# Storing the gates' running sums in DRAM by head instead of by chunk

## The chip, the cores and the metric

The kernel runs on one core of one Trainium2 chip. The metric is the device time of one execution in microseconds (us), the median of several runs. The profile quoted is of one further execution.

## What is computed

One step of a hybrid decoder layer for a prompt of 1024 tokens and eight sample tokens, with a model width of 1024 and 8 heads of 128. After a normalisation and modulation, one input projection feeds two branches: A, a gated short convolution, and B, a gated delta rule (conv on q, k and v, a decay per head and token, the delta rule, a gated norm). Both are projected, merged by gates, and go through one output projection. What the change touches is the decay in branch B, from the reference, cut:

```python
g = -exp(a_log) * softplus(alpha_raw + dt_bias)          # log decay, per token and head
...
gc = jnp.cumsum(g, axis=-1)                              # running sum within a chunk
causal = idx[:, None] >= idx[None, :]
decay = jnp.exp(jnp.where(causal, gc[..., :, None] - gc[..., None, :], -jnp.inf))
kb = k * beta[..., None]
a_mat = jnp.where(strict, einsum(kb, k) * decay, 0.0) + eye
sol = triangular_solve(a_mat, [v * beta, kb * exp(gc)])
attn_qk = einsum(q, k) * decay
q_dec = q * exp(gc)
# scan over the chunks: v_new = u - w S;  o = q_dec S + attn_qk v_new;  S = S exp(gc_last) + k_dec^T v_new
```

So each head needs its running sums twice: as a difference of every pair of tokens of a chunk (decay), and as a factor on q.

## The kernel before

The prompt is worked in 8 chunks (NC) of 128 tokens (C), for 8 heads (NH). Products with large weights run on TensorE (PE) as three products of split operands (xh, xl for the input, whi, wlo for the weights). The program has these stages: the start (norm, modulation); a long list of jobs, each one column block of 128 of the input projection, three groups of 344 columns accumulated in PSUM tiles pm_t; the products of branch A and of B's output; the output projection and the tail.

Branch B runs beside the list of jobs. Its work is written as generators ("strands"), one or more for each head, that are advanced in the gaps between the matmuls of the jobs (slot()). Which strand goes next, and so the order of instructions on each engine, is set while the program is built: the class Sched keeps an estimated clock for each engine, Paced charges each instruction an estimated cost to it, and a strand's next step is issued when its estimated time has come. For a DMA, Sched.dma charges a fixed time and one by bytes, whatever the shape of the transfer. On the chip each engine then works through its instructions in that order; an engine that waits for one instruction issues none behind it. All loads and stores but a few are issued on SP's queue (SY).

The running sums are made once, in ba_gen: a matmul with a triangle gives gc as 128 tokens x (8 chunks x 8 heads); a transpose on PE and a copy give gcr as 64 rows of 128 tokens; a DMA stores gcr to gsc, a DRAM scratch of 64 rows of 512 bytes (line 270). Two places read it for each head h through gc_rows(h), which makes 8 rows out of it and broadcasts them to all 128 partitions, 512 KB in SBUF:

- decay_gen (line 851) loads the tile DA; ACT adds the negative sum of the partition's own token to each of the 8 chunks (ACTIVATE DA<-DA,ngc, 8 for each head), DVE masks into DB and DA, ACT takes exponentials.
- delta_gen (line 982) loads the tile gcB; qd_gen takes its exponential on ACT and multiplies q by it on DVE.

delta_gen holds the rest of a head: the products of k and q; the inversion, whose blocks go through DRAM (sA, At, sT and back into Ts) with a long run of small DVE operations on Ts and Ttmp between; small products that finish the inverse (pa_t tiles with DB, Ts, T11); then the scan over the 8 chunks, in which PE, a DVE operation that writes X, PE again, an ACT copy that writes vn, and PE with vn follow each other. The PSUM tiles of branch B are pa_t, and the names in the profile are those of the tiles.

sample_gen, for the eight sample tokens, has a broadcast of the same size: it stores rT to rsc and reads it back to all partitions as rB, from one run of 4 KB in DRAM.

Of the kernel before, what the change touches and what calls it, by code (L numbers as in the profile page):

```python
# [8 lines left out]
F32 = mybir.dt.float32  # L9
# [7 lines left out]
P = 128  # L17
# [5 lines left out]
NH = 8  # L23
C = 128
NC = S // C
# [133 lines left out]
def hybrid_step(  # L159
# [9 lines left out]
    V, A, PE, GP, SY = (Paced(e, n, sched) for e, n in (  # L169
        (nc.vector, "V"), (nc.scalar, "A"), (nc.tensor, "PE"), (nc.gpsimd, "GP"), (nc.sync, "SY")))  # L170
# [9 lines left out]
    def ps_aux():  # L180
        return psum["pa"].tile([P, 512], F32, tag="pa", name="pa_t")

    def tt(out, a, b, op):
        V.tensor_tensor(out=out, in0=a, in1=b, op=op)

    def ts(out, a, s1, s2=None, op0=ALU.mult, op1=None):
        if s2 is None:
            V.tensor_scalar(out=out, in0=a, scalar1=s1, scalar2=None, op0=op0)
        else:
            V.tensor_scalar(out=out, in0=a, scalar1=s1, scalar2=s2, op0=op0, op1=op1)  # L190

    def stt(out, a, s, b, op0, op1):
        V.scalar_tensor_tensor(out=out, in0=a, scalar=s, in1=b, op0=op0, op1=op1)
# [6 lines left out]
    def act(out, in_, func, **kw):  # L200
        A.activation(out=out, in_=in_, func=func, **kw)
# [57 lines left out]
    gc = cpool.tile([P, NC, NH], F32, name="gc")  # L259
# [10 lines left out]
    gsc = dram.tile([NC * NH, C], F32, name="gsc")  # L270
# [11 lines left out]
    def transpose(out, in_):  # L282
        n = in_.shape[0]
        PE.transpose(out, in_, ident[:n, :n])
# [449 lines left out]
    def ba_gen():  # L734
        ap_ = bp
        ban = ap_.tile([P, 9, 16], F32, name="ban")
        GP.memset(ban, 0.0)
        pt = ps_aux()
        for i in range(9):
            n = P if i < 8 else NB  # L740
            transpose(pt[:n, 48 * i:48 * i + 48], ba[:, i * P:i * P + n])
        for n, i0, i1 in ((P, 0, 8), (NB, 8, 9)):
            pv = pt[:n, 48 * i0:48 * i1].rearrange("p (i n) -> p i n", n=48)
            V.tensor_copy(out=ban[:n, i0:i1, :], in_=pv[:, :, 0:16])
            tt(ban[:n, i0:i1, :], ban[:n, i0:i1, :], pv[:, :, 32:48], ALU.add)
        T4.give(ba_)
        al = ap_.tile([P, NH], F32, name="al")
        db = ap_.tile([P, NH], F32, name="db")
        SY.dma_start(out=al, in_=a_log.to_broadcast([P, NH]))
        SY.dma_start(out=db, in_=dt_bias.to_broadcast([P, NH]))  # L750
        act(beta, ban[:, :, 0:NH], AF.Sigmoid)
        yield
        xg = ap_.tile([P, 9, NH], F32, name="xg")
        u = ap_.tile([P, 9, NH], F32, name="u")
        sq = ap_.tile([P, 9, NH], F32, name="sq")
        pl = ap_.tile([P, 9, NH], F32, name="pl")
        tt(xg, ban[:, :, NH:16], db.unsqueeze(1).to_broadcast([P, 9, NH]), ALU.add)
        act(al, al, AF.Exp)
        stt(u, xg, -1.0, xg, ALU.mult, ALU.max)
        act(u, u, AF.Exp, scale=-1.0)  # L760
        ts(sq, u, 2.0, op0=ALU.add)
        V.reciprocal(out=sq, in_=sq)
        tt(u, u, sq, ALU.mult)
        tt(sq, u, u, ALU.mult)
        ts(pl, sq, 1.0 / 19)
        for n in (17, 15, 13, 11, 9, 7, 5, 3):
            stt(pl, pl, 1.0 / n, sq, ALU.add, ALU.mult)
        stt(pl, pl, 1.0, u, ALU.add, ALU.mult)
        ts(xg, xg, 0.0, op0=ALU.max)
        stt(xg, pl, 2.0, xg, ALU.mult, ALU.add)  # L770
        stt(xg, xg, -1.0, al.unsqueeze(1).to_broadcast([P, 9, NH]), ALU.mult, ALU.mult)
        yield

        pt = ps_aux()
        gv = xg[:, 0:8, :].rearrange("p c h -> p (c h)")
        PE.matmul(pt[:, 0:64], lhsT=triu, rhs=gv, start=True, stop=True)
        PE.matmul(pt[:, 64:128], lhsT=ones, rhs=gv, start=True, stop=True)
        gcf = gc.rearrange("p c h -> p (c h)")
        V.tensor_copy(out=gcf, in_=pt[:, 0:64])
        neg["gc"] = ngc = ap_.tile([P, NC, NH], F32, name="ngc")  # L780
        ts(ngc.rearrange("p c h -> p (c h)"), gcf, -1.0)
        tt(ekd.rearrange("p c h -> p (c h)"), pt[:, 64:128], gcf, ALU.subtract)
        act(egl.rearrange("p c h -> p (c h)"), pt[:, 64:128], AF.Exp)
        act(ekd, ekd, AF.Exp)
        act(egc, gc, AF.Exp)
        yield
        pt = ps_aux()
        transpose(pt[:64, 0:C], gcf)
        gcr = ap_.tile([64, C], F32, name="gcr")
        V.tensor_copy(out=gcr, in_=pt[:64, 0:C])  # L790
        SY.dma_start(out=gsc, in_=gcr)
        act(u[:NB, 0, :], xg[:NB, 8, :], AF.Exp)
        SY.dma_start(out=smp[0], in_=u[:NB, 0, :])
        SY.dma_start(out=smp[1], in_=beta[:NB, 8, :])
        SY.dma_start(out=gbs.rearrange("p a b h -> p (a b h)"),
                     in_=smp.rearrange("a b h -> (a b h)").unsqueeze(0).to_broadcast([P, 2 * NB * NH]))
        flags["ba"] = True
# [43 lines left out]

        jobs.append((w_in, c0, P, x_src, None, evac, after))

    gc_rows = lambda h: gsc.rearrange("(c h) i -> h c i", h=NH)[h].unsqueeze(0).to_broadcast([P, NC, C])
    waiting = set()

    def decay_gen(h, st):
# [968 lines left out]
    for g0, gn in GROUPS:  # L1816
# [5 lines left out]
        A.copy(out=ba[:, g0:g0 + gn], in_=ps[:48, :gn])  # L1822
    T4.give(wb_)
    start(ba_gen())
    run(jobs, 1, isp)
    products()
# [30 lines left out]
    for j in range(9):  # L1857
        i, n, xr, mh, ml, held = pre.pop(j)
# [33 lines left out]
        for half in range(2):  # L1892
            hs = slice(half * 512, (half + 1) * 512)
            stt(yt[:n, hs], yt[:n, hs], r, xr[:n, hs], ALU.mult, ALU.add)
            out = y_prompt[0, i * P:(i + 1) * P, hs] if i < 8 else y_sample[:, 0, hs]
# [38 lines left out]
```

## Time and profile before

| | |
|---|---|
| median of 3 runs | 1454.48 us (1453.16 to 1454.57) |
| the profiled execution | 1455.76 us; span from first to last instruction 1454.1 us |
| PE busy in the span | 1401.6 us, 96% |
| DVE, ACT, POOL busy | 994.0 us (68%), 673.0 us (46%), 38.2 us (3%) |
| mean granted clock of PE | 0.979 |
| DMA packets | 200271, of which 175774 under 2 KB; 165.99 MB |
| loads of DA and gcB from gsc | 8 and 8, 512 KB each |
| where they are issued | DA from 91.0 to 656.1 us, gcB from 126.3 to 689.4 us |

PE's busy time is that of pipelined matmuls and hides short waits. A wait that the profile lists is idle time of an engine, put down to what ended last before the instruction that follows. In rows of the profile every instruction has line 126, the helper that issues them, so tiles tell them apart. SPq is SP's instruction stream, which issues DMAs; a row of it is the issue, not the transfer.

### The profile page before, as it was taken

What the parts mean: (1) busy time and instruction counts of PE and PEld (TensorE: products, weight loads), DVE (VectorE), ACT (ScalarE), POOL (GpSimd) and SP (SyncE); (2) the same over time, 40 slices, a digit from 0 to 9 for tenths busy, and PEclk for the clock granted to TensorE, in tenths of its full rate; (3) what the DMA queues carried; (4) which work ended last, traced back from release to release, by engine and by line L of the source; (5) the groups of instructions that cost most, each with busy time, mean ns of one, the idle gap of its engine ahead of it and who ended that gap; (6) DMA issues with size and microseconds to landing.
All of it is one profiled execution on the core that took longest, in us unless ns stands there. A gap on an engine that the chain in (4) does not pass through costs nothing.

```text
span 1454.1 us, 26389 instructions
## 1 busy us (share of the span) xinstructions
PE 1401.6 (96%) x10246; PEld 1344.5 (92%) x10246; DVE 994.0 (68%) x2516; ACT 673.0 (46%) x1532; POOL 38.2 (3%) x95
## 2 busy tenths in 40 slices
PE   6999999989999999998899999999999999999997
PEld 4899988889989998988899999999999999999786
DVE  6766867576576867667573699877677877964553
ACT  6764755645473756555444344332222344532211
POOL 0000000000000000000000000000000120000000
PEclk9999998999899998999999999999999999999999
DMA  9523453223423422324343435432223684753221
GB/s 323 149 58 66 117 84 95 54 77 90 90 79 95 96 70 83 80 65 115 81 116 108 147 108 193 161 105 56 67 73 88 190 277 146 249 176 103 90 87 58
DMA packets 200271, 165.99 MB, mean 114 GB/s; under 512 B 34733, under 2 KB 175774, under 8 KB 200138
## 3 DMA queue, kind: packets, MB, share of 16 engines
q1 hardware_dynamic: 195592, 155.77, 37.3%
q0 software_dynamic: 4352, 8.46, 2.0%
q8 instruction: 80, 1.31, 0.4%
q14 instruction: 45, 0.37, 0.1%
q10 hardware_dynamic: 202, 0.08, 0.0%
HBM read 127.59 MB, written 36.91 MB: 113 GB/s over the span
## 4 chain that ended last, share of the span: by engine, by line
PE 77%; DVE 8%; DMA 8%; ACT 5%; issue 2%; SPq 1%; DVEq 0%; ACTq 0%
PE pm_t L126 52%; PE pa_t L126 22%; DMA DA<-gsc 4%; PE pb L126 2%; DVE wlo L126 1%; ACT junk L126 1%; DVE Ttmp L126 1%; DVE Ts L126 1%; DVE vT L126 1%; ACT DA L126 1%; DMA xs<-in_x_prompt_dram 1%; DVE kq L126 1%; DMA gcB<-gsc 1%; SPq L126 1%; ACT L126 1%
## 5 line engine op out<-in xcount | busy, mean ns | idle before, releaser
L126 PE MATMUL pm_t<-xh,whi 128*128 128x344 f32 (+1 forms) x1384 | 460.4, 333 | 0.0
L126 PE MATMUL pm_t<-xh,wlo 128*128 128x344 f32 (+1 forms) x1384 | 439.3, 317 | 0.5 <-DVE wlo L126 0.5
L126 PE MATMUL pm_t<-xl,whi 128*128 128x344 f32 (+1 forms) x1384 | 438.6, 317 | 0.0
L126 PEld LDWEIGHTS pm_t<-xh,whi 128*128 128x128 f32 x1384 | 265.9, 192 | 1.8 <-issue 0.2
L126 PEld LDWEIGHTS pm_t<-xl,whi 128*128 128x128 f32 x1384 | 266.0, 192 | 0.1
L126 PEld LDWEIGHTS pm_t<-xh,wlo 128*128 128x128 f32 x1384 | 265.0, 191 | 0.8 <-DVE wlo L126 0.7
L126 ACT CAST whi<-wr 128x1024 fp32r<-128x1024 f32 x60 | 62.8, 1047 | 133.4 <-PE pa_t L126 64.9
L126 DVE TENSOR_TENSOR wlo<-wraw,whi 128x512 fp32r<-128x512 f32 x112 | 75.8, 687 | 35.1 <-ACT whi L126 34.7
L126 ACT CAST whi<-wraw 128x512 fp32r<-128x512 f32 x112 | 67.9, 625 | 48.9 <-PE pm_t L126 43.4
L126 PE MATMUL pa_t<-thi,wlo 128*128 128x258 f32 x304 | 86.2, 283 | 0.2
L126 PE MATMUL pa_t<-thi,whi 128*128 128x258 f32 x304 | 85.9, 283 | 0.0
L126 PE MATMUL pa_t<-tlo,whi 128*128 128x258 f32 x304 | 85.9, 282 | 0.0
L126 PE MATMUL pm_t<-thi,wlo 128*128 128x258 f32 x304 | 85.7, 283 | 0.1
L126 PE MATMUL pm_t<-thi,whi 128*128 128x258 f32 x304 | 85.7, 282 | 0.0
L126 PE MATMUL pm_t<-tlo,whi 128*128 128x258 f32 x304 | 85.7, 282 | 0.0
L126 DVE TENSOR_TENSOR wlo<-wr,whi 128x1024 fp32r<-128x1024 f32 x60 | 73.2, 1220 | 11.1 <-ACT whi L126 10.9
L126 PE MATMUL pa_t<-xh,whi 128*128 128x258 f32 x256 | 72.4, 283 | 0.0
L126 PE MATMUL pa_t<-xh,wlo 128*128 128x258 f32 x256 | 72.3, 282 | 0.0
L126 DVE SCALAR_TENSOR_TENSOR kq<-raw,vecs,kq 128x528 f32<-128x528 f32 x96 | 70.0, 760 | 3.2 <-ACT kq L126 3.2
L126 PE MATMUL pa_t<-xl,whi 128*128 128x258 f32 x256 | 72.2, 282 | 0.0
L126 ACT ACT_TABLE_LOAD x39 | 50.0, 1283 | 36.1 <-DMA sg<-gBsc 6.5
L126 PE MATMUL pm_t<-yhi,whi 128*128 128x344 f32 x192 | 61.4, 320 | 0.0
(395 smaller groups left out, 3090.9 us busy)
## 6 DMA issues: line engine op xcount, KB each, us to landing
wraw<-in_w_in_dram SPq DMA_DIRECT2D x48, 512.0 KB
wr<-in_w_in_dram SPq DMA_DIRECT2D x64, 256.0 KB
aw<-in_ada_w_dram SPq DMA_DIRECT2D x16, 512.0 KB
gBsc<-gate SPq DMA_DIRECT2D x8, 516.0 KB
gAsc<-gate SPq DMA_DIRECT2D x8, 516.0 KB
txs<-phi SPq DMA_DIRECT2D x8, 516.0 KB
txs<-plo SPq DMA_DIRECT2D x8, 516.0 KB
yAsc<-acc SPq DMA_DIRECT2D x8, 516.0 KB
```

Source lines behind the costliest of these rows:

```text
L126: r = f(*args, **kw)
```

## The change

A second copy of the running sums, gch, is made with heads outside and chunks inside; the transpose takes gch in place of gc. The rows of gsc then lie by head, then by chunk, and gc_rows(h) reads 8 rows that follow each other, one run of 4 KB, where it read 8 rows of 512 bytes that lie 4 KB apart. What is computed stays the same. The charges of Sched are unchanged; the copy is charged like any other, and so moves the estimated clock of DVE a little.

```diff
         V.tensor_copy(out=gcf, in_=pt[:, 0:64])
+        gch = ap_.tile([P, NH, NC], F32, name="gch")
+        V.tensor_copy(out=gch, in_=gc.rearrange("p c h -> p h c"))
         neg["gc"] = ngc = ap_.tile([P, NC, NH], F32, name="ngc")
...
-        transpose(pt[:64, 0:C], gcf)
+        transpose(pt[:64, 0:C], gch.rearrange("p h c -> p (h c)"))
...
-    gc_rows = lambda h: gsc.rearrange("(c h) i -> h c i", h=NH)[h].unsqueeze(0).to_broadcast([P, NC, C])
+    gc_rows = lambda h: gsc.rearrange("(h c) i -> h c i", h=NH)[h].unsqueeze(0).to_broadcast([P, NC, C])
```

Three places of the order of instructions change; everywhere else only numbers in names do. On DVE, in ba_gen (kq is the convolution of the first head's q that runs beside it, ngc and ekd are made of the sums), as a piece of the difference:

```order
 L126 COPY gc<-pa_t 128x64
 L126 SCALAR_TENSOR_TENSOR kq<-raw_720,vecs,kq 128x528
+L126 COPY gch<-gc 128x64
 L126 TENSOR_SCALAR ngc<-gc 128x64
 L126 TENSOR_TENSOR ekd<-pa_t,gc 128x64
-L126 SCALAR_TENSOR_TENSOR kq<-raw_720,vecs,kq 128x528 x3
+L126 SCALAR_TENSOR_TENSOR kq<-raw_720,vecs,kq 128x528 x2
 L126 COPY gcr<-pa_t 64x128
+L126 SCALAR_TENSOR_TENSOR kq<-raw_720,vecs,kq 128x528
```

The copy stands ahead of ngc, and gcr, from which the sums are stored, now runs ahead of the last kq operation.

On SP, from the store of the sums on. Before:

```order
L126 DMA gsc<-gcr 64x128
L126 DMA DA<-gsc 128x8x128
L126 DMA wraw<-in_w_in_dram 128x8x128
L126 DMA gBsc<-gate 128x1032
L126 DMA wraw<-in_w_in_dram 128x8x128 x2
L126 DMA gcB<-gsc 128x8x128
L126 DMA rsc<-sm_rT 8x128
L126 DMA sA<-DB 32x8x32
L126 DMA rB<-rsc 128x1024
```

And now:

```order
L126 DMA gsc<-gcr 64x128
L126 DMA DA<-gsc 128x1024
L126 DMA wraw<-in_w_in_dram 128x8x128
L126 DMA gBsc<-gate 128x1032
L126 DMA wraw<-in_w_in_dram 128x8x128 x2
L126 DMA gcB<-gsc 128x1024
L126 DMA rsc<-sm_rT 8x128
L126 DMA sA<-DB 32x8x32
L126 DMA rB<-rsc 128x1024
```

The order is the same; the two loads from gsc are now written with one run in each partition, like rB, and so are the 14 later ones.

On ACT, at the first head's additions (gate is the copy of a job's result out of PSUM):

```order
 L126 CAST whi<-wraw 128x512
-L126 ACTIVATE DA<-DA,ngc 128x128 x4
-L126 COPY gate<-pm_t 128x344
-L126 ACTIVATE DA<-DA,ngc 128x128 x4
+L126 ACTIVATE DA<-DA,ngc 128x128 x3
+L126 COPY gate<-pm_t 128x344
+L126 ACTIVATE DA<-DA,ngc 128x128 x5
 L126 ACTIVATE vT<-vT 128x1056
```

The gate copy moves ahead of one addition.

## The prediction

> **What bounds the kernel now.** I read the table of stretches first, then the chain that ended last, then the waits of ACT and of PE, and last the order of time around one stall. The table of stretches has one row for each stretch: its length, busy time of PE, weight loads, DVE, ACT and POOL with the number of instructions, the granted clock, the busy share of the DMA engines and GB/s.
>
> ```profile
> 61.00:822.00 761.00, 728.77 (x5395) 707.04 (x5396) 493.59 (x1631) 415.09 (x1153) 21.67 (x54) 0.96 0.34 87
> 822.00:1454.00 632.00, 623.95 (x4547) 598.82 (x4545) 458.14 (x778) 214.60 (x312) 11.62 (x16) 1.00 0.42 133
> ```
>
> All broadcasts of the running sums are issued between 61 and 822 us, where the eight heads run. PE is the busiest engine there, yet it stands idle for 761.00 - 728.77 = 32.2 us and is granted 0.96 of its clock, which is 4% of 761 us, some 30 us more at most. So about 60 us of that stage are not PE's work at full pace; behind 822 us nothing of the change runs. The question is how much of the 60 us the broadcasts cause. The chain of work that ended last puts it at 4% of the span on one of the two, 1% on the other:
>
> ```profile
> PE pm_t L126 52%; PE pa_t L126 22%; DMA DA<-gsc 4%; PE pb L126 2%; DVE wlo L126 1%; ACT junk L126 1%; DVE Ttmp L126 1%; DVE Ts L126 1%; DVE vT L126 1%; ACT DA L126 1%; DMA xs<-in_x_prompt_dram 1%; DVE kq L126 1%; DMA gcB<-gsc 1%; SPq L126 1%; ACT L126 1%
> ```
>
> In order of time its DMA pieces (start, us from issue to landing) are these; the last two are transfers with rows of 4 KB from later stages, for comparison:
>
> ```profile
> 190.35 13.51 DMA DA<-gsc
> 244.09 9.79 DMA gcB<-gsc
> 310.36 8.44 DMA DA<-gsc
> ...
> 460.27 8.41 DMA DA<-gsc
> ...
> 656.10 9.59 DMA DA<-gsc
> 692.31 6.35 DMA Ts<-sT
> ...
> 1176.79 7.03 DMA yraw<-yAsc
> ...
> 1191.00 4.00 DMA sg<-gBsc
> ```
>
> A broadcast takes 8.4 to 9.8 us, and 13.5 us when another one (gcB, issued at 184.38) is still ahead of it in SP's queue. Who waits, on ACT in that stage (total us, times, longest):
>
> ```profile
> ACT DA L126 <- DMA DA<-gsc: 38.2, 7, 6.7
> ...
> ACT gcB L126 <- DMA gcB<-gsc: 12.9, 3, 6.9
> ...
> ACT L126 <- DMA gcB<-gsc: 5.7, 1, 5.7
> ...
> ACT rB L126 <- DMA rB<-rsc: 3.8, 1, 3.8
> ```
>
> ACT issues its work in order, so behind such a wait stand the copies that PE needs. The waits of PE in the same stage:
>
> ```profile
> PE pa_t L126 <- ACT vn L126: 15.5, 8, 4.5
> PE pa_t L126 <- ACT DB L126: 5.1, 2, 2.6
> PE pa_t L126 <- DVE os_all L126: 2.7, 1, 2.7
> PE pa_t L126 <- DVE X L126: 2.6, 2, 2.1
> PE pa_t L126 <- ACT junk L126: 2.5, 1, 2.5
> ```
>
> These five rows hold 15.5 + 5.1 + 2.7 + 2.6 + 2.5 = 28.4 of the 32.2 us. None names a DMA; the order of time shows how they hang on one. This is the stall at 315 us, on SP's queue, ACT and PE (start, us, instruction, idle time before it and what ended it):
>
> ```profile
> 310.36 0.36 SPq L126 DMA_DIRECT2D DA<-gsc  x1
> ...
> 318.82 0.98 ACT L126 ACTIVATE DA<-DA,ngc 128x128 f32<-128x128 f32 x3 [6.30 <-DMA DA<-gsc]
> 319.71 0.24 ACT L126 COPY vn<-pa_t 128x128 f32<-128x128 f32 x1
> ...
> 315.14 0.32 PE L126 MATMUL pm_t<-xh,wlo 128*128 128x344 f32 x1
> 320.01 0.49 PE L126 MATMUL pa_t<-vn,kd 128*128 128x128 f32 x2 [4.55 <-ACT vn L126]
> ```
>
> ACT waits 6.30 us for the broadcast of one head, three of its additions run, then the small copy vn of another head, for which PE has waited since 315.3. Followed back in the same way, the other stalls of PE over 0.8 us between 190 and 710 us end at a broadcast too: directly, through Ts<-sT queued behind one, or through DVE work held up by one.
>
> **The change, part by part.** *The transfer.* It goes from 128 x 8 runs of 512 bytes to 128 runs of 4 KB, from the same 4 KB of DRAM to all partitions. The trace has no such transfer from gsc, but rB<-rsc has the same form, 128x1024 from one run of 4 KB. It made ACT wait in one of its eight calls, the broadcast DA in seven of eight. That one call, and two stretches in which a broadcast DA (with 512-byte runs) and an rB each had the queue almost alone, and one of a weight load in 512-byte runs:
>
> ```profile
> 141.51 0.40 SPq L126 DMA_DIRECT2D rB<-rsc  x1
> ...
> 145.78 0.40 ACT L126 ACTIVATE rB<-rB,sm_ks 128x128 f32<-128x128 f32 x1 [3.82 <-DMA rB<-rsc]
> ```
>
> ```profile
> 399.80:408.40 8.60, 8.60 (x58) 8.42 (x58) 6.10 (x15) 3.35 (x15) 0.20 (x1) 1.00 0.24 69
> 570.60:572.60 2.00, 2.00 (x23) 1.79 (x22) 2.00 (x7) 1.48 (x2) 0.53 (x1) 1.00 0.77 248
> 524.50:526.00 1.50, 1.50 (x13) 1.50 (x12) 0.00 (x0) 0.45 (x1) 0.00 (x0) 1.00 1.02 289
> ```
>
> From issue to use rB took 145.78 - 141.51 = 4.3 us. The bounds for the new broadcast are the 4.00 us of sg<-gBsc and the 7.03 us of yraw<-yAsc; I take 4.3, since rB alone has the same shape and the same repeated source. So each broadcast lands 4.1 to 5.5 us earlier, what is queued behind it (Ts<-sT, weights, sA) with it, and the one of 13.5 us more. With 7.03 it would be 1.4 to 2.8 us.
>
> The Trainium skill, page "DMA: Bandwidth & Descriptors", section "Specifications", speaks against this: it gives 512 bytes as the run from which a transfer is at line rate, so longer runs would bring nothing. The weight load above agrees with it (289 GB/s in runs of 512 bytes), the broadcast (69 GB/s, same runs) does not. By that rule the time would stay at 1454.5.
>
> What makes the broadcast slow is then not its run length alone, but that all partitions fetch the same eight short runs; rB fetches one same long run at 248 GB/s, and so I expect the new form to do.
>
> *The idle time.* In the stall above the broadcast would land at 310.36 + 4.3 = 314.7, the three additions end at 315.7, vn follows at 315.9, against PE's need at 315.3: of 4.55 us some 0.6 remain. The others are shorter than the 4.1 us gained, or about as long. Nothing says that PE finds all else in time once it is earlier: I count 85% of the 28.4 us, 24 us. What is late next is the chain of small products, DVE and ACT copies of the running head. ACT's waits for the first two broadcasts, before 190 us, have no stall of PE behind them and are worth nothing.
>
> *The clock.* After its stalls PE runs at half its clock. The periods at 0.50 in that stage (three of 3.41 us are left out here, the sum has all nine):
>
> ```profile
> 197.71:201.12 3.41, 3.41 (x14) 3.19 (x15) 3.41 (x10) 0.16 (x1) 0.00 (x0) 0.50 1.07 55
> 231.84:242.08 10.24, 9.91 (x53) 9.34 (x54) 8.98 (x36) 3.54 (x8) 0.53 (x1) 0.50 0.36 111
> ...
> 368.37:382.02 13.65, 13.65 (x73) 12.66 (x73) 7.96 (x20) 1.16 (x2) 0.73 (x2) 0.50 0.19 45
> ...
> 559.52:569.76 10.24, 7.75 (x71) 7.15 (x69) 4.21 (x10) 4.74 (x13) 0.52 (x1) 0.50 0.41 132
> 634.61:641.44 6.83, 6.83 (x34) 6.34 (x34) 4.07 (x24) 4.77 (x11) 0.73 (x2) 0.50 0.24 71
> 668.74:672.15 3.41, 3.41 (x16) 3.41 (x15) 3.16 (x6) 2.75 (x5) 0.00 (x0) 0.50 0.00 0
> sum 58.01, PE 55.19 PEld 51.96 DVE 39.52 ACT 26.83 POOL 2.51; mean PE 6.13 PEld 5.77 DVE 4.39 ACT 2.98 POOL 0.28
> ```
>
> Five periods of 3.41 us stand right behind a stall and cost half of their length: 5 x 1.7 = 8.5 us. The one from 368.37 has no stall ahead of it (many tiny matmuls of the inversion seem to be enough) and stays. The three of 10.24, 10.24 and 6.83 us have both; half of their cost of 13.7 us goes, 6.8 us. Of these 15.3 us I count two thirds, 10 us, because shorter stalls that remain may still trip it.
>
> The Trainium skill, "TensorE: Matmul & The Clock Gate", Part 1, says that the clock halves after an idle window of about 3.4 us and returns after as long a busy one. The length of the periods agrees, the threshold does not: stalls of 2.1 to 2.7 us are followed by half clock here. By its rule only the stalls over 3.4 us would give clock back, at most 3 x 1.7 us, and the time would be 1426.
>
> *The added copy and the order.* gch is one DVE copy; the copy of the same shape and the operation that now runs behind gcr are these, with ACT's wait for the first broadcast some 10 us later:
>
> ```profile
> 85.73 0.21 DVE L126 COPY gc<-pa_t 128x64 f32<-128x64 f32 x1
> ...
> 86.77 2.11 DVE L126 SCALAR_TENSOR_TENSOR kq<-raw,vecs,kq 128x528 f32<-128x528 f32 x3
> ...
> 99.51 1.28 ACT L126 ACTIVATE DA<-DA,ngc 128x128 f32<-128x128 f32 x4 [3.15 <-DMA DA<-gsc]
> ```
>
> It costs 0.2 us of DVE once (0.1 to 0.4 with its strided read). Behind it wait ngc and ekd, and the transpose on PE, which now waits for gch. gcr moves ahead of one of three kq operations of 0.7 us, so the first broadcast is issued some 0.5 us sooner and that kq operation ends 0.5 us later; ACT, which needs it, idles 3.15 us soon after, so the cost is nothing; the earlier landing takes that cover away, so I count 0.5 us. On ACT a gate copy trades places with one addition of 0.4 us: nothing. SP issues the same transfers in the same order, and the issue itself costs it 0.36 against 0.40 us.
>
> *Sum.* 24 + 10 - 0.5 = 33.5 us, say 34, off the span of 1454.1 us: 1420. The profiled execution took 1455.76 us, 1.7 us around the span; the median of the three runs is 1454.48, 1.3 us under it. So 1455.8 - 34 - 1.3 = 1420.5 us.
>
> **The rivals.** *Half of it.* With the broadcasts early, PE reaches the next wait that was hidden behind them: the chain of eight steps in each head, or the At, sT and Ts transfers that are not changed. For it speaks that the order was set by estimated times, against it that ACT and DVE wait mostly for PE in this stage, and that PE's other waits there add to only 32.2 - 28.4 = 3.8 us. The same comes out if a broadcast still takes near 7 us. If only 12 us of idle time and 4 us of clock go, the time is 1438; I let this case run from 1430 to 1447.
>
> *No change.* The short run is not the cause, and 4 KB from gsc comes as slowly as eight runs did: 1454.5. The rate of rB speaks against it.
>
> *Slower.* All 16 DMA engines now start every partition at the same address at once. If that were served worse than eight addresses and each broadcast took the 13.5 us that one did, the ten late ones would each add 4 us: 1494. It decides from a landing over 9.6 us; again rB, which does this, lands in 4.3.
>
> *All of it.* 28.4 us of idle time and 15.3 us of clock: 1411; with every idle us and every half of the three long periods 32.2 + 8.5 + 13.7 = 54 us, 1400.
>
> **How the numbers follow.** The likeliest case, 1408 to 1430, gets 0.67; half of it 0.20; more than that (under 1408) 0.04; no change 0.06; slower 0.03. A range from 1408 to 1441 leaves out the last three and the upper part of the second, about 2 in 10. A measurement of this kernel tells 0.2% (2.9 us) from no change: faster 0.91, same 0.06, slower 0.03.
>
> **What would show it.** In the profile of the changed kernel ACT's waits for DA<-gsc and gcB<-gsc should fall from 56.8 us to under 15; the chain should lose most of its 4% on DA<-gsc; PE's idle time between 61 us and the end of the heads from 32 to under 10 us; the granted clock there rise from 0.96 to 0.97 or 0.98; a broadcast should show 4 to 5 us from issue to use. Wrong in the first step: waits as long as before. Wrong in the second: short waits for gsc, but PE's idle time kept up by rows with vn, X or DB that follow no DMA. Wrong in the third: idle time gone, and the clock still at 0.96.

## The result, and the profile after

The changed kernel takes 1405.09 us (1402.08 to 1405.82), the kernel before 1454.53 us in the same comparison: a ratio of 0.965 (95% interval 0.961 to 0.968), 49.4 us less. The forecast was 1420.5 us with a range from 1408 to 1441; the direction was right, and the gain was larger than its range allowed. The profiled execution took 1405.82 us, its span is 1404.1 us, 50.0 us shorter than before. Medians are of the runs that agree: one run of the kernel with a single slow broadcast, below, took 2712.53 us and is left out.

The table of stretches, with the first cut where PE has done as many matmuls as before had at 822 us (5395 there, 5394 here; columns as in the prediction):

```profile
61.00:772.00 711.00, 707.45 (x5394) 689.59 (x5395) 493.48 (x1631) 416.78 (x1154) 23.77 (x54) 0.99 0.33 93
772.00:1404.00 632.00, 623.62 (x4549) 598.80 (x4546) 458.44 (x778) 214.43 (x312) 11.61 (x16) 1.00 0.42 133
```

The stage of the heads is 761 - 711 = 50 us shorter, the rest 632 us in both: all of the gain lies where the broadcasts are. PE's idle time there fell from 32.2 to 711.00 - 707.45 = 3.55 us, and its busy time, for the same matmuls, from 728.8 to 707.5 us, nearly all of which is the clock (20.8 us, worked out below). The chain of the work that ended last, by line, no longer has DMA DA<-gsc among its first entries, where it had 4% of the span:

```profile
PE pm_t L126 62%; PE pa_t L126 25%; PE pb L126 2%; DMA xs<-in_x_prompt_dram 1%; ACT junk L126 1%; DVE wlo L126 1%; DVE Ttmp L126 0%; DVE Ts L126 0%; DMA yraw<-yAsc 0%; DVE acc L126 0%; DMA yAsc<-acc 0%; SPq L126 0%; ACT whi L126 0%; DMA DA<-gsc 0%; DMA wr<-in_w_in_dram 0%
```

ACT's waits for the broadcasts in that stage (total us, times, longest) are 6.8 + 2.4 = 9.2 us, from 56.8:

```profile
ACT DA L126 <- DMA DA<-gsc: 6.8, 4, 2.4
...
ACT L126 <- DMA gcB<-gsc: 2.4, 2, 2.1
```

and these four rows are all of PE's listed waits there, 3.4 us in sum; the rows with DB, os_all, X and junk are gone, and no new one has come:

```profile
PE pa_t L126 <- ACT vn L126: 1.5, 4, 0.7
PE pm_t L126 <- ACT last_q L126: 1.1, 1, 1.1
PE pa_t L126 <- DVE S L126: 0.5, 2, 0.3
PE pa_t L126 <- DVE DA L126: 0.3, 1, 0.3
```

The stall that the prediction followed at 315 us is, in order of time, now this:

```profile
294.64 0.33 SPq L126 DMA_DIRECT2D DA<-gsc  x1
...
299.23 0.99 ACT L126 ACTIVATE DA<-DA,ngc 128x128 f32<-128x128 f32 x3 [2.43 <-DMA DA<-gsc]
...
300.12 0.24 ACT L126 COPY vn<-pa_t 128x128 f32<-128x128 f32 x1
...
300.42 0.49 PE L126 MATMUL pa_t<-vn,kd 128*128 128x128 f32 x2 [0.68 <-ACT vn L126]
```

From issue to use the broadcast takes 299.23 - 294.64 = 4.59 us instead of 318.82 - 310.36 = 8.46, ACT waits 2.43 instead of 6.30, and PE 0.68 instead of 4.55. Of the nine periods at half clock one is left in the stage:

```profile
347.28:360.93 13.65, 13.65 (x72) 12.66 (x73) 7.91 (x19) 1.16 (x2) 0.73 (x2) 0.50 0.19 47
```

In half-clock periods PE was busy for 55.19 us before (the sum row in the prediction) and is for 13.65 now; half of the difference is 20.8 us. With 32.2 - 3.55 = 28.7 us of idle time that makes 49.5 of the 50 us. The work of the stage at full clock is the same in both: 728.77 - 55.19 / 2 = 701.2 us, and 707.45 - 13.65 / 2 = 700.6.

### The profile page after: what moved, and what is told of

It is laid out like the page before. It is cut to its first block, busy times and chain, and to the rows that moved or that the text cites. A ratio compares the mean times of both kernels' runs of the same rounds, so it can differ in the third digit from the quotient of the medians.

```text
span 1404.1 us, 26390 instructions
## 1 busy us (share of the span) xinstructions
PE 1379.4 (98%) x10246; PEld 1326.8 (94%) x10246; DVE 994.1 (71%) x2517; ACT 674.0 (48%) x1532; POOL 40.3 (3%) x95
## 3 DMA queue, kind: packets, MB, share of 16 engines
q0 software_dynamic: 4352, 8.46, 2.1%
## 4 chain that ended last, share of the span: by engine, by line
PE 90%; DVE 4%; DMA 2%; ACT 2%; issue 1%; SPq 0%; DVEq 0%; ACTq 0%
PE pm_t L126 62%; PE pa_t L126 25%; PE pb L126 2%; DMA xs<-in_x_prompt_dram 1%; ACT junk L126 1%; DVE wlo L126 1%; DVE Ttmp L126 0%; DVE Ts L126 0%; DMA yraw<-yAsc 0%; DVE acc L126 0%; DMA yAsc<-acc 0%; SPq L126 0%; ACT whi L126 0%; DMA DA<-gsc 0%; DMA wr<-in_w_in_dram 0%
## 5 line engine op out<-in xcount | busy, mean ns | idle before, releaser
L126 PE MATMUL pm_t<-xh,whi 128*128 128x344 f32 (+1 forms) x1384 | 454.4, 328 | 0.0
L126 PE MATMUL pm_t<-xh,wlo 128*128 128x344 f32 (+1 forms) x1384 | 434.4, 314 | 0.0
L126 PE MATMUL pm_t<-xl,whi 128*128 128x344 f32 (+1 forms) x1384 | 433.6, 313 | 0.0
L126 PEld LDWEIGHTS pm_t<-xh,whi 128*128 128x128 f32 x1384 | 261.6, 189 | 1.6
L126 PEld LDWEIGHTS pm_t<-xl,whi 128*128 128x128 f32 x1384 | 261.6, 189 | 0.1
L126 PEld LDWEIGHTS pm_t<-xh,wlo 128*128 128x128 f32 x1384 | 260.9, 189 | 0.1
L126 ACT ACTIVATE junk<-pa_t 128x128 f32<-128x128 f32 x192 | 54.0, 281 | 16.1 <-PE pa_t L126 13.8
```

Of the source, the lines that this page charges most:

```text
L126: r = f(*args, **kw)
```

## Experiments

Two things were to be settled: what made the eight short runs slow, since the prediction gave a cause that it had not tested, and how much a late broadcast costs PE. Before in these comparisons took 1452.4 to 1454.9 us. Where a kernel is called the changed one, its order and gch are kept.

**Is it the short runs that all partitions share?** Rows of gsc 1 KB apart, so that each broadcast is again 128 x 8 runs of 512 bytes:

```diff
-    gsc = dram.tile([NC * NH, C], F32, name="gsc")
+    gsc = dram.tile([NC * NH, 2 * C], F32, name="gsc")
...
-        SY.dma_start(out=gsc, in_=gcr)
+        SY.dma_start(out=gsc[:, 0:C], in_=gcr)
...
-    gc_rows = lambda h: gsc.rearrange(...)[h].unsqueeze(0)...
+    gc_rows = lambda h: gsc.rearrange(...)[h][:, 0:C].unsqueeze(0)...
```

> The changed kernel (copy gch, its order of instructions, sums stored by head), but each row of 512 bytes lies in a slot of 1 KB, so that a broadcast again fetches 8 runs of 512 bytes for each partition, now 1 KB apart instead of 4 KB. Theory A (all partitions fetch the same short runs, and each fetch of the same place has its price): a broadcast takes 8 to 10 us from issue to use as before, the time is 1454, within 4. Theory B (the distance of 4 KB between the runs made it slow): 4 to 5 us, time 1405. Theory C (the number of runs has its price, wherever they lie): as A, 1454. By A and C the copy gch and the moved kq operation are worth under 1 us, so that this kernel and the one before differ by less than that.

1406.13 us (1404.05 to 1412.61), ratio 0.968 (0.963 to 0.973): as fast as one run. The prediction's cause (A) and the number of runs (C) fall, and the distance (B) is left. The next two took the other sides: runs of their own for each partition (the decays are then made of other numbers), and longer runs at a distance.

```diff
+    gc_rows = lambda h: w_in[0, :, h * C:(h + 1) * C].rearrange("(k p) c -> p k c", p=P)   # runs of its own for each partition
```

> The changed kernel, but the broadcasts DA and gcB are fed from the input projection's weights: 128 x 8 runs of 512 bytes that all differ, as in the weight loads. The decay is computed from wrong numbers; all instructions and sizes are the same. Theory A: 4 to 5 us from issue to use, time 1405, within 4. Theory B: as fast, 1405 (the runs lie 41 KB apart). Theory C: 8 to 10 us, 1454.

1404.33 us (1400.69 to 1406.78), as A and B had it; C, the number of runs, falls again. (41 KB is the distance from one partition's run to the next one's; the eight runs of a partition lie 128 rows of the weights apart.)

```diff
-    gsc = dram.tile([NC * NH, C], F32, name="gsc")
+    gsc = dram.tile([NH * 4, 4 * C], F32, name="gsc")      # 4 runs of 1 KB; in the other kernel [NH * 2, 8 * C], 2 runs of 2 KB
...
+    gc_rows = lambda h: gsc.rearrange("(h g) i -> h g i", h=NH)[h][:, 0:2 * C].unsqueeze(0).to_broadcast([P, 4, 2 * C])   # in the other [:, 0:4 * C], [P, 2, 4 * C]
```

The parts left out copy and store the sums in two (four) pieces, so that two (four) chunks stand side by side in a row.

> The changed kernel with the sums in slots such that a broadcast fetches 4 runs of 1 KB for each partition, the slots 2 KB apart (one more small store DMA and one more small copy, once). Theory A and C: half the fetches of before, which moved 1024 runs in some 7 us: 512 runs in 3.5 us and a start of about 1.3, 4.8 us to use; that is 0.5 us more than the 4 KB form, and with stalls of PE that were at most 4.6 us long next to nothing comes back: 1405 to 1410. Theory B: 1405.

> The same with 2 runs of 2 KB for each partition, the slots 4 KB apart. Theory A and C: 256 fetches, 1.8 us, now less than the bytes take; 4.3 us to use, time 1405, within 3. Theory B (distance of 4 KB): two runs 4 KB apart, some way back to slow, 1410 to 1430.

1406.5 us (1401.19 to 1407.47) and 1404.96 us (1400.82 to 1407.48). Two runs of 2 KB that start 4 KB apart are fast, so a distance of 4 KB is no harm by itself; theory B in the form that it had there (1410 to 1430) missed.

**Distance, order, or spread?** The kernel before, in its own order and without gch, with 64 bytes added to each row, so that its runs lie 4.5 KB apart; and the changed kernel with its rows 4 KB apart:

```diff
-    gsc = dram.tile([NC * NH, C], F32, name="gsc")
+    gsc = dram.tile([NC * NH, C + C // 8], F32, name="gsc")   # in before; in the changed kernel [NC * NH, 8 * C]
...                                                           # store and load of [:, 0:C] as with 1 KB
```

> The kernel before (its order, no gch, sums by chunk, then by head), with rows of gsc padded to 576 bytes, so that the eight 512-byte runs of a broadcast lie 4.5 KB apart instead of 4 KB. Theory 'distance' (eight short runs exactly 4 KB apart are served slowly): broadcasts land in 4 to 5 us, 1405 (1400 to 1410). Rival 'spread' (runs spread over 32 KB are slow, whatever the step): as before, 1454. Rival 'order' (the gain came with the new order and gch, the broadcasts only followed): 1454 too, but with landings of 4 to 5 us.

1404.88 us (1403.9 to 1406.78), ratio 0.966 (0.965 to 0.967). The pad alone brings the whole gain, as theory 'distance' had it. The order of the change, gch and the single run add nothing to it that can be measured.

> The changed kernel, with the rows of gsc 4 KB apart again (order and gch of the changed kernel kept, every broadcast 128 x 8 runs of 512 bytes). Theory 'distance': landings of 8 to 10 us, ACT's waits for gsc back at some 55 us, 1454 (1448 to 1458). Rival 'order': 1405 to 1415 with ACT's waits near 10 us.

1447.44 us (1445.16 to 1449.25), ratio 0.995 (0.994 to 0.996). The gain is gone but for 7 us, as 'distance' had it, though just under its range (1448 to 1458). With the runs 2 KB apart in the changed kernel (rows of 4 * C), and 8 KB apart in the kernel before (rows of 2 * C):

> The changed kernel, with the rows of gsc 2 KB apart (runs of 512 bytes, 1024 in a broadcast). Theory 'channels' (addresses a multiple of 4 KB apart are served by one place, so that 2 KB apart two places share the work): landings half way, some 5.5 to 6.5 us, and 1408 to 1425. Rival 'only 4 KB and its multiples': 1405, landings of 4 us. Rival 'powers of two from 2 KB': 1447, landings of 8 to 10 us.

1415.02 us (1412.67 to 1415.84), ratio 0.972 (0.967 to 0.977): within what 'channels' gave, and as neither rival had it. From the third head on its DA take 5.1 to 6.4 us from issue to use.

> The kernel before (its order, no gch), with rows of gsc 1 KB apart, so that the eight runs of a broadcast lie 8 KB apart instead of 4 KB. Theory 'channels': multiples of 4 KB are all alike: landings of 8 to 10 us, 1447 to 1457. Rival 'only 4 KB': 1405, landings of 4 to 5 us.

1536.42 us (1535.78 to 1537.22), ratio 1.056 (1.050 to 1.062): slower than before by 84 us, which neither theory had. The first broadcast DA, alone in the queue, shows why. One row of the table of stretches from each (last column GB/s), with the runs 8 KB, 4 KB, 2 KB and 1 KB apart:

```profile
92.50:93.50 1.00, 1.00 (x8) 1.00 (x7) 0.79 (x1) 1.00 (x2) 0.00 (x0) 1.00 0.22 45
```

```profile
92.50:93.50 1.00, 1.00 (x8) 1.00 (x8) 0.17 (x3) 1.00 (x2) 0.00 (x0) 1.00 0.34 86
```

```profile
92.50:93.50 1.00, 1.00 (x8) 1.00 (x7) 0.17 (x3) 1.00 (x2) 0.00 (x0) 1.00 0.58 173
```

```profile
92.50:93.50 1.00, 1.00 (x9) 1.00 (x8) 0.29 (x3) 1.00 (x2) 0.00 (x0) 1.00 1.06 324
```

45, 86, 173, 324 GB/s: each doubling of the distance about halves the rate. With 4.5 KB, in the padded kernel before, it is back:

```profile
93.00:94.00 1.00, 1.00 (x8) 1.00 (x7) 0.47 (x1) 1.00 (x2) 0.00 (x0) 1.00 1.03 310
```

The broadcast of head 3, from issue to ACT's first use, with the runs 8 KB apart (16.8 us) and 4.5 KB apart (4.3 us), each from its own trace:

```profile
333.99 0.36 SPq L126 DMA_DIRECT2D DA<-gsc  x1
...
350.78 0.99 ACT L126 ACTIVATE DA<-DA,ngc 128x128 f32<-128x128 f32 x3 [14.64 <-DMA DA<-gsc]
```

```profile
295.71 0.36 SPq L126 DMA_DIRECT2D DA<-gsc  x1
...
300.02 0.99 ACT L126 ACTIVATE DA<-DA,ngc 128x128 f32<-128x128 f32 x3 [2.16 <-DMA DA<-gsc]
```

The Trainium skill, "DMA: Bandwidth & Descriptors", section "Latency and other measured facts", has a row of the same kind: copies whose rows lie a large power of two apart (512 KiB to 8 MiB) run at down to half of their rate, a pad of 4 KiB restores it, a pad of 192 bytes does not, and aliasing of memory channels is given as an inference. The loss that grows with the distance and the cure by a pad agree in kind; the distances here are a hundred times smaller, the loss from 1 to 8 KB is about a half for each doubling, and a pad that moves the runs by 512 bytes is enough.

**Does it need the sharing?** Runs of its own for each partition, 4 KB apart, from an input with rows of 4 KB; the same with eight runs shared by all partitions; and eight shared runs 64 KB apart:

```diff
+    gc_rows = lambda h: x_prompt[0, :, h * C:(h + 1) * C].rearrange("(p k) c -> p k c", p=P)   # own runs
... in the second kernel
+    gc_rows = lambda h: x_prompt[0, h * NC:(h + 1) * NC, h * C:(h + 1) * C].unsqueeze(0).to_broadcast([P, NC, C])   # shared, 4 KB
... in the third kernel
+    gc_rows = lambda h: x_prompt[0, 0:128, h * C:(h + 1) * C].rearrange("(k r) c -> r k c", r=16)[h].unsqueeze(0).to_broadcast([P, NC, C])   # shared, 64 KB
```

> The changed kernel, with DA and gcB loaded from the input x_prompt (rows of 4 KB): every partition fetches eight runs of its own of 512 bytes, 4 KB apart; the decays are then made of other numbers. Theory 'distance alone': slow as eight shared runs, landings of 8 to 10 us, 1440 to 1455. Rival 'distance and sharing' (it needs that all 128 partitions fetch the same runs): landings of 4 to 5 us, 1405.

1405.0 us (1401.89 to 1409.89), ratio 0.966 (0.961 to 0.971): the rival, 'distance and sharing'.

> As the kernel with eight runs of its own for every partition out of x_prompt (rows of 4 KB), but all 128 partitions fetch the same eight runs, 4 KB apart; decays from other numbers. Theory 'distance and sharing': slow again, 85 GB/s, landings of 8 to 10 us, 1440 to 1455. Rival 'tensor' (x_prompt lies elsewhere or in another state than gsc, and 4 KB of it is fast however it is read): 4 to 5 us, 1405.

1445.4 us (1443.88 to 1448.07), ratio 0.994 (0.992 to 0.996): slow again, so it is not the tensor.

> The same, with the eight shared runs 64 KB apart. Theory 'one place' (from 8 KB on all eight runs fall on one place, at 43 GB/s as with 8 KB): landings of 13 to 15 us, 1530 or more. Rival 'spread again' (farther address bits spread the runs over places, which would also explain why 1024 runs of their own over 4 MB were fast): 4 to 6 us, 1405 to 1420.

1446.35 us (1444.31 to 1458.55), ratio 0.996 (0.994 to 0.998). The rates of one broadcast gcB in these three, in the same order:

```profile
128.50:130.00 1.50, 1.50 (x11) 1.50 (x10) 0.00 (x0) 1.48 (x2) 0.00 (x0) 1.00 0.88 259
```

```profile
128.50:130.00 1.50, 1.50 (x12) 1.50 (x11) 0.00 (x0) 1.48 (x2) 0.00 (x0) 1.00 0.27 85
```

```profile
128.50:130.00 1.50, 1.50 (x11) 1.50 (x10) 0.36 (x3) 1.01 (x2) 0.00 (x0) 1.00 0.36 81
```

Same tensor, same distance, same run: 259 GB/s with own runs, 85 with shared ones. So it takes both: runs at such a distance, and all partitions at the same few of them. The slow kernel reads eight addresses, the fast one 1024, over 4 MB; whether it counts that the addresses are few or that they are shared, these runs do not tell apart. At 64 KB neither theory holds: the rate is that of 4 KB, not that of 8 KB, so the rule is not simply "the farther the worse".

**How much does a late broadcast cost?** A second copy of the sums with rows 4 KB apart (gsp), read by the DA of one head, by all DA, or by all gcB of the changed kernel; the order on the engines is that of the changed kernel but for one more store:

```diff
+    gsp = dram.tile([NC * NH, 8 * C], F32, name="gsp")
...
         SY.dma_start(out=gsc, in_=gcr)
+        nc.sync.dma_start(out=gsp[:, 0:C], in_=gcr)
...
+    gc_slow = lambda h: gsp.rearrange("(h c) i -> h c i", h=NH)[h][:, 0:C].unsqueeze(0).to_broadcast([P, NC, C])
...
-        SY.dma_start(out=DA, in_=gc_rows(h))
+        SY.dma_start(out=DA, in_=(gc_slow if h == 3 else gc_rows)(h))   # all DA, or all gcB, in the other two
```

> The changed kernel, with one broadcast of the sixteen (DA of head 3, issued near 295 us) from a second copy of the sums with rows 4 KB apart; one more store. It then lands near 303 instead of 299.2 us. Theory 'idle and clock': PE stalls some 4 us and then runs 3.41 us at half clock, 4 + 1.7 = 5.7 us: 1410.5. Rival 'idle only': 4 us, no period at half clock, 1409. Rival 'absorbed' (what follows in the head catches up): under 1407, as the changed kernel's 1405.

1408.34 us (1406.94 to 1409.14), 3.2 us over the changed kernel, whose own runs spread over 3.7 us. That is nearest to 'idle only', but the trace shows more than idle time. The stall is there as foreseen:

```profile
294.25 0.36 SPq L126 DMA_DIRECT2D DA<-gsp  x1
...
302.82 0.98 ACT L126 ACTIVATE DA<-DA,ngc 128x128 f32<-128x128 f32 x3 [6.44 <-DMA DA<-gsp]
303.71 0.24 ACT L126 COPY vn<-pa_t 128x128 f32<-128x128 f32 x1
...
304.01 0.80 PE L126 MATMUL pa_t<-vn,kd 128*128 128x128 f32 x2 [4.69 <-ACT vn L126]
```

and so is a period at half clock right at it; the stage is in the second row:

```profile
302.98:309.81 6.83, 5.80 (x23) 5.81 (x24) 2.83 (x8) 4.80 (x17) 0.00 (x0) 0.50 0.16 34
61.00:772.00 711.00, 703.75 (x5392) 686.19 (x5393) 493.12 (x1631) 416.28 (x1154) 23.87 (x54) 1.00 0.33 93
```

PE idles 711.00 - 703.75 = 7.25 us, 3.7 more than in the changed kernel, and the period costs 5.80 / 2 = 2.9 us. But the 13.65 us at half clock from 347 us did not come in this execution, which is worth 6.8 us, and the stage is as long as without the slow broadcast. So the trace shows idle and clock, at 6.6 us together, and the medians show 3.2; how often the later period stays away can't be told from one profile.

> The changed kernel, with all eight DA broadcasts from a second copy with rows 4 KB apart, and all gcB from the run of 4 KB. Theory 'each by its waits': in the kernel before ACT waited 38.2 us for DA of 56.8 in all, so two thirds of the 50 us come back: 1438 (1433 to 1444). Rival 'queue' (DA is only late because gcB stands before it in the queue): under 1425. Rival 'either alone does it': 1448 or more.

1426.86 us (1426.48 to 1428.14), ratio 0.981 (0.979 to 0.982). 21.8 us over the changed kernel, not 33: neither what its share of the waits gives (1438), nor what the rival 'either alone' gives (1448), and just over the bound of 'queue' (1425).

```profile
61.00:794.00 733.00, 712.27 (x5397) 692.84 (x5397) 493.76 (x1632) 416.16 (x1154) 21.67 (x54) 0.98 0.33 91
307.63:314.46 6.83, 6.09 (x24) 6.09 (x25) 2.92 (x8) 4.62 (x17) 0.00 (x0) 0.50 0.14 24
539.74:549.98 10.24, 8.10 (x71) 7.50 (x69) 4.59 (x10) 5.18 (x13) 0.90 (x2) 0.50 0.63 133
642.13:648.96 6.83, 5.96 (x24) 5.96 (x24) 4.86 (x14) 4.48 (x13) 0.00 (x0) 0.50 0.04 16
```

Idle 20.7 us, 17.2 more than in the changed kernel; half-clock work 20.2 us against 13.65, half of which is 3.3 us more: 20.4 of the 22 us that the stage is longer.

> The counterpart of the kernel with slow DA broadcasts: all eight gcB from a second copy with rows 4 KB apart, all DA from the run of 4 KB. Theory 'additive': all sixteen slow cost 42 us (1447.4 against 1405.1), the DA alone 22 us, so gcB alone costs 20: 1425. Rival 'each by its waits' (ACT's waits for gcB were 18.6 us of 56.8 in the kernel before): a third, 14 us: 1419. Rival 'hidden' (gcB is loaded well ahead of its use, and matters only where a DA stands behind it in the queue, which is now fast): under 1412.

1426.27 us (1423.51 to 1426.83), ratio 0.980 (0.975 to 0.984): 21.2 us over the changed kernel, additive (21.8 + 21.2 against 42.3 for all sixteen). Here ACT waits only 11.8 us for gcB, but Ts<-sT, behind gcB in the queue, makes ACT wait 5.7 us more:

```profile
ACT gcB L126 <- DMA gcB<-gsp: 11.8, 3, 7.4
ACT L126 <- DMA Ts<-sT: 5.7, 1, 5.7
```

So half of what the slow broadcasts cost belongs to gcB, which had a third of the waits.

## Why the prediction was right or wrong

**The transfer: right in size, wrong in cause.** 4.3 us were taken from rB, 4.6 us were measured at head 3. The sentence "all partitions fetch the same eight short runs" named one of two conditions. The sharing, or the few addresses that come with it, is needed (259 against 85 GB/s at the same distance), the distance of 4 KB too (324 GB/s at 1 KB with the same sharing), the short run is not what counts. The number came out because the new layout removes the distance as well; that is luck. By the cause given a pad would have brought nothing; 64 bytes for each row brought as much as the long run. The rule of 512 bytes that the prediction weighed against it (the Trainium skill, "DMA: Bandwidth & Descriptors", "Specifications") holds here for shared runs 1 KB or 4.5 KB apart and fails at 2, 4 and 8 KB.

**The idle time: the discount to 85% was wrong.** 28.4 us were found to hang on broadcasts and 24 counted; 28.7 went. The kernel with slow DA and the one with slow gcB bring 21.8 and 21.2 us back, together 43.0 of the 49.4 us, so the reading of the waits was right, down to the stall of 4.55 us, for which 0.6 us was forecast to remain and 0.68 did. Nothing became late next: the rival "half of it" would have shown as rows of PE's waits, and those that are left hold 3.4 us.

**The clock: the step that failed most.** 10 us were counted, 20.8 measured. The five short periods went, as counted (8.5 us), but the three long ones went whole, not by half (13.7, not 6.8), and nothing of it was lost to shorter stalls, for which a third had been taken off. Half of these eight periods' lengths is 22.2 us; as PE is idle in 2.8 us of them, 20.8 is what the clock paid.

The third taken off was the clear error, as no stall was left that could cost it. The halving was not without ground. Its reason was that the inversion's tiny matmuls can trip the clock alone. They can: the 13.65 us stays in the changed kernel, and one of the three long periods, the one from 559.52, does not follow its stall as the prediction had it. It begins among the tiny matmuls, and PE waits only from 563.26 on:

```profile
559.11 2.13 PE L126 MATMUL pa_t<-Ts 32*32 32x32 f32 x48
...
562.77 0.49 PE L126 MATMUL pm_t<-xh,wlo 128*128 128x344 f32 x1
565.75 1.94 PE L126 MATMUL pa_t<-DB 64*64 64x64 f32 x16 [2.49 <-ACT DB L126]
```

At the same place the changed kernel with rows 1 KB apart, whose broadcasts are fast, is at half clock with PE busy throughout:

```profile
527.05:533.88 6.83, 6.83 (x35) 6.34 (x34) 4.24 (x9) 5.09 (x12) 1.84 (x2) 0.50 0.56 172
```

So that this period stayed away from the profile of the changed kernel is in part the luck of one execution. The other period in tiny matmuls comes and goes too, and is not as fixed as the prediction had it: where the changed kernel has 13.65 us, the padded kernel before has 13.65, the changed one with rows 1 KB apart 3.41, and the one with a single slow DA none. In all, the profiles of the seven kernels whose broadcasts are fast hold 3.4 to 13.65 us at half clock in this stage, against 58.0 before; the changed kernel's 13.65 is the top of that, so 20.8 us is no lucky figure for the whole.

**The rule of the clock gate.** By the Trainium skill, "TensorE: Matmul & The Clock Gate", Part 1, only idle windows of some 3.4 us would halve the clock; the prediction put 1426 to that. The single slow broadcast, a stall of 4.69 us, agrees with it. 20.8 us of clock, where the stalls over 3.4 us account for three times 1.7 us at most, do not. Nor does this stall of the kernel before, the third longest, behind which the clock stays at 1.00:

```profile
701.23 0.49 PE L126 MATMUL pa_t<-vn,kd 128*128 128x128 f32 x2 [3.61 <-ACT vn L126]
```

**Copy and order: right.** 0.5 us was counted; the padded kernel before, without both, takes 1404.88 us against 1405.09. With slow broadcasts the new order was 7 us faster than the old (1447.4 against 1454.9); why is open: the rows also lie elsewhere, and one profile of each, with 44.4 and 58.0 us at half clock, does not settle it.

**The sum.** 28.7 + 20.8 = 49.5 us against 24 + 10 - 0.5. Both terms were measured out well from the trace and then reduced, the idle time by 15% and the clock from 22.2 to 10 us, for waits that might come next and for half clock that might stay, though the trace showed only 3.8 us of other waits. The undiscounted sum of the same rows, put among the rivals as "all of it" (1411, at the utmost 1400), had the right time between its ends.

## What to carry to other kernels

When a transfer that many partitions read from the same few addresses is slow, look at the distance between these addresses first: a pad that takes it off a power of two (here of 2 KB or more) may bring what a new layout brings, without a copy or a new order. Where every stall of a stage has been followed back to one cause, and the trace shows no other wait of that size, count the stalls whole, and with them the half-clock work behind them. And the waits for a transfer do not say what it costs: what is queued behind it can carry as much, as with gcB.

## What the runs showed of the hardware

The rate of a shared broadcast of 512 KB in runs of 512 bytes depends on the distance of the runs: 324 GB/s at 1 KB, 173 at 2 KB, 86 at 4 KB, 45 at 8 KB, 310 at 4.5 KB, and 81 at 64 KB in another tensor. That looks as if each doubling puts the eight addresses on half as many places that serve them, and 64 KB brings some of them apart again; which addresses share a place was not tried further, and that it is a place in DRAM is only argued. The time follows with growing weight: 512 KB at these rates take 1.6, 3.0, 6.1 and 11.7 us. In the changed kernel's order the first three give 1406, 1415 and 1447 us, so a us more for each broadcast costs 6 us at first and then 11; in the order of before, 6.1 and 11.7 us give 1452 and 1536, 15 us for each, nearly as many as there are broadcasts.
